# Tile 47's results leave in four transfers of two queues instead of with their neighbours

## The chip, the cores and the metric

The kernel runs on one core of a Trainium2 chip. The metric is the device time of one execution in microseconds. A second figure, the span, is the time from the first to the last instruction of the profiled execution.

## The reference

```python
x, weight, add_value: float32 of (16, 512, 1024), (1024, 768), (16, 512, 768); scale = 0.1

def reference(x, weight, scale, add_value):
    return (scale * np.matmul(x, weight) + add_value).astype(np.float32)
```

It is one product of 8192 x 1024 by 1024 x 768. With all inputs and the output in float32, some 87 MB have to be moved between memory and the core.

## The kernel before

The 8192 rows are cut into 64 tiles of 128 rows. A tile is not 128 neighbouring rows: `BLOCKS` splits the matrix into three blocks of 24, 24 and 16 tiles, and in a block each of the 128 partitions holds so many neighbouring rows, one for each tile. A transfer of n neighbouring tiles therefore moves 128 pieces, one for each partition, of n rows: 4 KB a row for `x`, 3 KB for `add_value` and for the result.

All transfers are issued by SyncE, on one queue, in the order written out by hand in `STREAM` (lines 22 to 25). `x0+4` loads tiles 0 to 3 of `x`, `w0+8` the weight, `a0+8` loads tiles 0 to 7 of `add_value`, and `o32+16` stores the results of tiles 32 to 47. `sync_engine` goes through the list and waits, ahead of each transfer, for what it needs: free slots for a load, finished results for a store. The last entry, `o62+2`, is issued at line 261, after a barrier of all engines that closes the main section (line 255).

On chip the work of a tile goes through these steps:

- `xs` (16 slots) receives tiles of `x`. In `mover`, ScalarE and GpSimd convert them to bf16 into one of two buffers `va`, four tiles at a time: one such step of four is called a move, there are 16, each engine does half of the quadrants of 32 partitions (line 166), and the semaphores `by_act` and `by_pool` count its conversions. The first four moves stand by themselves; the other twelve are a loop of three rounds (line 174).
- VectorE transposes two tiles at a time into `xt` (line 190) and counts `turned`. A move waits for `turned` before it overwrites its buffer.
- TensorE multiplies the transposed tile with the weight, in pieces of 512 and 256 columns (lines 248 and 222), and counts `done`.
- VectorE's `finish` (line 199) takes a pair of tiles, scales the product, adds `ao` (32 slots, into which `add_value` was loaded) and writes the result to the same slots of `ao`. The semaphore `made` counts finished tiles; it starts from the constant `MADE`. There are 32 pairs.

A store of tiles up to `last` waits for `made` to reach `MADE + last`. Tile 47 lies in a slot of `ao` that no later load uses.

Of the kernel before, what the change touches and what calls it, by code (L numbers as in the profile page):

```python
# [7 lines left out]
P = 128  # L8
BLOCKS = ((0, 24), (24, 24), (48, 16))
G = 8  # L10
X_SLOTS = 16
# [5 lines left out]
MOVE = 4  # L17
O_LANES = 4
HALVED = (0, 1)
FETCH = 128  # L20

STREAM = """
    x0+4 w0+8 x4+8 a0+8 x12+4 a8+8 x16+8 a16+8 x24+8 a24+8 x32+8 o0+8 o8+8 a32+8 x40+8
    a40+8 x48+8 x56+4 o16+8 o24+8 a48+4 x60+4 a52+4 a56+8 o32+16 o48+8 o56+6 o62+2
"""


# [7 lines left out]
def kernel(  # L35
# [17 lines left out]
    T = M // P  # L53
# [4 lines left out]
    def blocks(flat):  # L58
        return [(s, g, flat[P * s:P * (s + g), :].rearrange("(p t) n -> p t n", t=g))
                for s, g in BLOCKS]  # L60

    x_v, add_v, out_v = blocks(x_f), blocks(add_f), blocks(out_f)
    w_v = weight.rearrange("(p r) n -> p r n", p=P)

    def rows(view, s, n):
        for first, g, block in view:
            if first <= s and s + n <= first + g:
                return block[:, s - first:s - first + n, :]
        raise ValueError((s, n))
# [5 lines left out]
    ao = const.tile([P, A_SLOTS, N], fp32, name="ao")  # L75
# [10 lines left out]
    by_act, by_pool, pool_go, turned, casts, done, made = (  # L86
        tc.alloc_semaphore(name)
        for name in ("by_act", "by_pool", "pool_go", "turned", "casts", "done", "made"))
    TURNED = MOVE * VA_BUFS
    MADE = TURNED + MM_BUFS  # L90

    def slots(t, n):
        k = (t + G) % A_SLOTS
        assert k + n <= A_SLOTS
        return slice(k, k + n)

    def transfer(eng, op, s, n):
        if op == "w":
            return eng.dma_start(ao[:, s:s + n, :], w_v[:, s:s + n, :])  # L99
        if op == "x":  # L100
            k = s % X_SLOTS
            return eng.dma_start(xs[:, k:k + n, :], rows(x_v, s, n))  # L102
        if op == "a":
            return eng.dma_start(ao[:, slots(s, n), :], rows(add_v, s, n))
        return eng.dma_start(rows(out_v, s, n), ao[:, slots(s, n), :])

    def sync_engine(eng):
        loads, stores, known = [], [], {}

        def need(sem, value):  # L110
            if known.get(id(sem), 0) < value:
                eng.wait_ge(sem, value)
                known[id(sem)] = value

        for op, s, n in stream[:-1]:
            last = s + n
            if op == "w":
                sem = w_sem
            elif op == "x":
                lane = s % X_SLOTS // MOVE  # L120
                if last > X_SLOTS:
                    moved = 8 * (last - X_SLOTS) // MOVE
                    need(by_act, moved)
                    need(by_pool, moved)
                if n == 2 * MOVE:
                    eng.sem_inc(x_sem[lane + 1], 16)
                sem = x_sem[lane]
            elif op == "a":
                if loads:
                    need(a_sem, 16 * len(loads))  # L130
                if slots(s, n).start < KJ:
                    need(casts, KJ)
                if s >= A_SLOTS:
                    for i, (a, b) in enumerate(stores):
                        if a < last - A_SLOTS and s - A_SLOTS < a + b:
                            need(o_sem[i % O_LANES], 16 * (i // O_LANES + 1))
                if s % G:
                    sem = a_late
                else:
                    sem = a_sem  # L140
                    loads.append((s, n))
            else:
                i = len(stores)
                if i >= O_LANES:
                    need(o_sem[i % O_LANES], 16 * (i // O_LANES))
                need(made, MADE + last)
                sem = o_sem[i % O_LANES]
                stores.append((s, n))
            transfer(eng, op, s, n).then_inc(sem, 16)

    def mover(eng, copy, parity, count, go=None):
        if go is None:
            eng.preload_act_table(mybir.ActivationFunctionType.Copy)  # L153

        def move(q, step, landed, freed):
            eng.wait_ge(x_sem[q], landed)
            if freed is not None:
                eng.wait_ge(turned, freed)
            if go is not None:
                eng.sem_inc(go, 1)  # L160
            k = MOVE * q
            src = xs[:, k:k + MOVE, :].rearrange("p i (b k) -> p i b k", b=4)
            for t in range(0, MOVE, step):
                for a in (parity, parity + 2):
                    for b in range(4):
                        copied = copy(va[q % VA_BUFS][32 * b:32 * b + 32, t:t + step, a, :],  # L166
                                      src[32 * a:32 * a + 32, t:t + step, b, :])
                        if step == MOVE or b % 2:
                            copied.then_inc(count, 1)

        for q in range(X_SLOTS // MOVE):
            move(q, MOVE // 2 if q in HALVED else MOVE, 16,
                 MOVE * (q + 1) if q >= VA_BUFS else None)
        with eng.Fori(32, T + 1, X_SLOTS) as i:
            for q in range(X_SLOTS // MOVE):
                move(q, MOVE, i, i + (4 * q - 12) if q < 3 else i)

    def vector_engine(eng):
        ao_g = ao.rearrange("p (g t) n -> p g t n", t=G)
# [73 lines left out]
    for eng in (nc.scalar, nc.gpsimd):  # L253
        eng.addr_align(FETCH, offset=0, max_nops=0)
    with tc.tile_critical(no_gpsimd_drain=True):  # L255
        sync_engine(nc.sync)
        mover(nc.scalar, nc.scalar.copy, 0, by_act)
        mover(nc.gpsimd, nc.gpsimd.tensor_copy, 1, by_pool, pool_go)
        vector_engine(nc.vector)
        tensor_engine(nc.tensor)  # L260
# [36 lines left out]
```

## Time and profile before

| | |
|---|---|
| time, median of 3 runs | 209.57 us (209.47 to 209.66) |
| the profiled execution | 209.42 us, of which the span is 207.6 us |
| granted TensorE clock, mean | 0.978 |
| bytes moved | 87.05 MB, 419 GB/s over the span |
| busy, share of the span | TensorE 82%, GpSimd 67%, ScalarE 66%, VectorE 59% |

Times in quoted rows are microseconds from the start of the span. A row of the timeline gives the start, the duration, the engine and line, the operation, and in brackets the idle time before it and what ended it. A row of a DMA view gives the buffers, the issuing queue, the number of issues, their size and the time from issue to landing; SPq is SyncE's queue, L105 a store, L104 a load of `add_value`, L102 a load of `x`. POOL is GpSimd, DVE VectorE, ACT ScalarE, PE TensorE.

### The profile page before, as it was taken

To read this page: it belongs to the slowest core of one execution; us is meant where nothing else is said; L and a number is where in the kernel's file an instruction comes from. 1 tells how busy PE (TensorE), PEld (TensorE's weight loads), DVE (VectorE), ACT (ScalarE), POOL (GpSimd) and SP (SyncE) were. 2 spreads that over 40 slices of the span, in tenths; PEclk is the share of its full clock that TensorE was granted. 3 is DMA by queue.
4 is the path that set the end of the run, shared out by engine and by line. 5 is a ranking of instruction groups with operands and counts; after the bars stand their busy time and mean duration, and the time that the engine had idled before them with its cause. 6 is when DMAs were issued, how large, how long until landed. Compare 5 with 4: busy or idle time off the path is not lost.

```text
span 207.6 us, 2250 instructions
## 1 busy us (share of the span) xinstructions
PE 170.7 (82%) x1024; PEld 50.8 (24%) x512; DVE 123.0 (59%) x66; ACT 137.8 (66%) x145; POOL 138.3 (67%) x148
## 2 busy tenths in 40 slices
PE   0001993699999999999999999999999899999800
PEld 0000230123223333333333333333333233333200
DVE  0038304937677767776777677767774867777320
ACT  2494199999596969696969079999696959100000
POOL 0399299999797969696969179999796959200000
PEclk9999999699999999999999999999999999999995
DMA  6999999999999999899999999999999999998994
GB/s 224 458 432 410 448 455 404 455 455 404 404 473 436 420 388 505 350 421 440 436 431 447 404 450 459 404 420 436 436 421 428 412 455 469 455 445 355 434 420 173
DMA packets 4034, 87.05 MB, mean 419 GB/s; under 512 B 448, under 2 KB 448, under 8 KB 576
## 3 DMA queue, kind: packets, MB, share of 16 engines
q1 hardware_dynamic: 4032, 87.03, 98.0%
q14 instruction: 2, 0.02, 0.0%
HBM read 61.87 MB, written 25.17 MB: 419 GB/s over the span
## 4 chain that ended last, share of the span: by engine, by line
PE 59%; DMA 26%; POOL 5%; DVE 4%; issue 2%; SPq 0%; DVEq 0%; POOLq 0%
PE mm L248 39%; PE mm L222 20%; DMA xs<-in_x_dram 11%; DMA out_dram<-ao 10%; DMA ao<-in_add_value_dram 5%; POOL va L166 5%; DVE xt L190 2%; DVE ao L199 2%; SPq L99 0%; SPq L102 0%; DVEq L199 0%; DVEq L196 0%; POOLq L160 0%; DVEq L188 0%; SPq L292 0%
## 5 line engine op out<-in xcount | busy, mean ns | idle before, releaser
L248 PE MATMUL mm<-w_bf,xt 128*128 128x512 bf16 x512 | 170.3, 385 | 26.0 <-DVE w_bf L183 20.2
L166 POOL CAST va<-xs 32x1024 bf16<-32x1024 f32 (+1 forms) x144 | 138.1, 959 | 39.1 <-DMA xs<-in_x_dram 18.6
L166 ACT CAST va<-xs 32x1024 bf16<-32x1024 f32 (+1 forms) x144 | 136.5, 948 | 38.4 <-DMA xs<-in_x_dram 20.5
L222 PE MATMUL mm<-w_bf,xt 128*128 128x256 bf16 x512 | 141.4, 276 | 0.0
L199 DVE SCALAR_TENSOR_TENSOR ao<-mm,ao 128x1536 f32 (+1 forms) x32 | 56.2, 1755 | 58.7 <-PE mm L222 46.2
L248 PEld LDWEIGHTS mm<-w_bf,xt 128*128 128x128 bf16 x512 | 50.8, 99 | 145.4 <-issue 138.4
L190 DVE STREAM_TRANSPOSE xt<-va 128x1024 f32<-128x1024 f32 x32 | 65.2, 2037 | 16.9 <-POOL va L166 16.9
L183 DVE CAST w_bf<-ao 128x3072 bf16<-128x3072 f32 x2 | 4.3, 2170 | 0.0
L153 ACT ACT_TABLE_LOAD x1 | 1.3, 1283 | 1.3 <-SPq L255 1.3
L278 POOL MEMSET const-float32-0.0<- 128x1 f32 x1 | 0.1, 98 | 0.2 <-issue 0.2
L278 POOL MEMSET const-bfloat16-1.0<- 128x1 bf16 x1 | 0.1, 100 | 0.0
L278 POOL MEMSET const-uint8-127<- 128x1 uint8 x1 | 0.1, 98 | 0.0
L278 POOL MEMSET const-float32-1.0<- 128x1 f32 x1 | 0.1, 97 | 0.0
## 6 DMA issues: line engine op xcount, KB each, us to landing
xs<-in_x_dram SPq DMA_DIRECT2D x6, 4096.0 KB, 20.5
ao<-in_add_value_dram SPq DMA_DIRECT2D x7, 3072.0 KB, 17.0
out_dram<-ao SPq DMA_DIRECT2D x5, 3072.0 KB, 22.4
xs<-in_x_dram SPq DMA_DIRECT2D x4, 2048.0 KB, 14.3
out_dram<-ao SPq DMA_DIRECT2D x1, 6144.0 KB, 29.9
ao<-in_weight_dram SPq DMA_DIRECT2D x1, 3072.0 KB, 14.0
ao<-in_add_value_dram SPq DMA_DIRECT2D x2, 1536.0 KB, 9.9
out_dram<-ao SPq DMA_DIRECT2D x1, 2304.0 KB, 11.5
```

Source lines behind the costliest of these rows:

```text
L153: eng.preload_act_table(mybir.ActivationFunctionType.Copy)
L166: copied = copy(va[q % VA_BUFS][32 * b:32 * b + 32, t:t + step, a, :], src[32 * a:32 * a + 32, t:t + step, b, :])
L183: eng.tensor_copy(w_bf[:, s:s + n, :], ao[:, s:s + n, :]).then_inc(casts, n)
L190: eng.transpose(xt[:, 2 * half:2 * half + 2, :, :].rearrange("p i c (a m) -> p i c a m", a=4), pairs.rearrange("p i a (k c) -> p i c a k", ...
L199: eng.scalar_tensor_tensor(a, mm[:, q:q + 2, 0:N], float(scale), a, op0=mybir.AluOpType.mult, op1=mybir.AluOpType.add).then_inc(made, 2)
L222: return eng.add_instruction(mybir.InstMatmult(name=nc.get_next_instruction_name(), engine=eng.engine, ins=[eng.lower_ap(weights), eng.low ...
L248: eng.matmul(mm[:, q, 0:CUT], piece, w_bf[:, j, 0:CUT], **flags)
L278: nc = _bacc.Bacc("TRN2", target_bir_lowering=False, num_devices=1)
```

## The change

`o32+16` becomes `o32+15`, and tile 47 is stored by four transfers, cut by rows (partitions): SyncE issues the first 6 rows right after `o32+15`; GpSimd issues the next 5, then 105, then 12. GpSimd does so between its last two moves, once tile 47 is finished. For that the loop of the movers is turned by one: three moves stand ahead of it, a round begins with the fourth, and the last move stands behind it. Each of the four transfers has its own semaphore, and ScalarE waits for all of them at its end. By the change's account the rows are dealt so that DMA engine 4 gets three of the 128.

```diff
+SPREAD = 47
+SPREAD_ROWS = (("SP", 6), ("Pool", 5), ("Pool", 105), ("Pool", 12))
...
-    a40+8 x48+8 x56+4 o16+8 o24+8 a48+4 x60+4 a52+4 a56+8 o32+16 o48+8 o56+6 o62+2
+    a40+8 x48+8 x56+4 o16+8 o24+8 a48+4 x60+4 a52+4 a56+8 o32+15 o48+8 o56+6 o62+2
...
+    spread_sem = [tc.alloc_semaphore(f"spread{i}") for i in range(len(SPREAD_ROWS))]
+
+    def spread(eng, name):
+        first = 0
+        for (by, n), sem in zip(SPREAD_ROWS, spread_sem):
+            if by == name:
+                eng.dma_start(rows(out_v, SPREAD, 1)[first:first + n],
+                              ao[first:first + n, slots(SPREAD, 1), :]).then_inc(sem, 16)
+            first += n
+        assert first == P
...
             transfer(eng, op, s, n).then_inc(sem, 16)
+            if op == "o" and last == SPREAD:
+                need(made, MADE + SPREAD + 1)
+                spread(eng, "SP")
...
-        for q in range(X_SLOTS // MOVE):
+        for q in range(3):
             move(q, MOVE // 2 if q in HALVED else MOVE, 16,
                  MOVE * (q + 1) if q >= VA_BUFS else None)
-        with eng.Fori(32, T + 1, X_SLOTS) as i:
-            for q in range(X_SLOTS // MOVE):
-                move(q, MOVE, i, i + (4 * q - 12) if q < 3 else i)
+        with eng.Fori(16, T, X_SLOTS) as i:
+            move(3, MOVE, i, i)
+            for q in range(3):
+                move(q, MOVE, i + 16, i + 4 * (q + 1))
+        if go is not None:
+            eng.wait_ge(made, MADE + SPREAD + 1)
+            spread(eng, "Pool")
+        move(3, MOVE, T, T)
+        if go is None:
+            for sem in spread_sem:
+                eng.wait_ge(sem, 16)
```

## The prediction

> **What bounds the kernel now.** I began with the page's sums and its lines on DMA, because a kernel that moves 87 MB in 208 us may simply be moving bytes.
>
> ```profile
> span 207.6 us, 2250 instructions
> ...
> DMA packets 4034, 87.05 MB, mean 419 GB/s; under 512 B 448, under 2 KB 448, under 8 KB 576
> ...
> q1 hardware_dynamic: 4032, 87.03, 98.0%
> ```
>
> The sixteen DMA engines are busy 98% of the span, and there is one queue, SyncE's. So every microsecond that an engine of the sixteen moves bytes counts, and compute counts only where it would leave that queue empty. The counts also give the shape of the last transfer: 576 packets under 8 KB less 448 under 512 B are 128 pieces, the 128 rows of o62+2 (two tiles, 6 KB a row), and 128 over 16 engines is 8 each.
>
> Next, who waits at the end: the waits of SyncE from 175 us on.
>
> ```profile
> SPq L292 <- DMA out_dram<-ao: 7.5, 1, 7.5
> SPq L255 <- DVEq L255: 4.7, 1, 4.7
> ```
>
> Line 255 is the barrier after which the last transfer is issued, and it ends with VectorE; line 292 is the end of the program, which waits 7.5 us for stores. So the end is a store landing. How the sixteen engines come to that end is seen in busy time by stretch: width, each engine's busy time, then the TensorE clock, the DMA share and GB/s.
>
> ```profile
> 203.60:204.40 0.80, 0.00 (x0) 0.00 (x0) 0.00 (x0) 0.00 (x0) 0.00 (x0) 0.50 1.02 430
> 204.40:205.09 0.69, 0.00 (x0) 0.00 (x0) 0.00 (x0) 0.00 (x0) 0.00 (x0) 0.50 0.40 162
> 205.09:206.24 1.16, 0.00 (x0) 0.00 (x0) 0.00 (x0) 0.00 (x0) 0.00 (x0) 0.50 0.06 27
> 206.24:207.63 1.39, 0.00 (x0) 0.00 (x0) 0.00 (x0) 0.00 (x0) 0.00 (x0) 0.50 0.00 0
> ...
> 177.00:199.00 22.00, 19.70 (x122) 5.79 (x60) 13.62 (x8) 0.45 (x1) 0.70 (x1) 1.00 0.99 428
> ```
>
> This is the reading on which all else rests. Until 204.40 us all sixteen are busy; from 205.09 to 206.24 the share is 0.06, one sixteenth. One engine alone works for the last 1.16 us. The DMA view of just that stretch counts its packets:
>
> ```profile
> DMA packets 6, 0.03 MB, mean 27 GB/s; under 512 B 1, under 2 KB 1, under 8 KB 6
> ```
>
> Five pieces of 6 KB and one of some bytes: 1.16/5 = 0.23 us for 6 KB, thus 0.115 us for a 3 KB row at that rate. The fifth row of the stretches agrees: 428 GB/s over 16 engines is 26.75 GB/s, and 3,072 B take 0.115 us in large pieces too. No other engine starts a piece after 205.09, so every other one has ended by 205.32. The late one is 0.92 to 1.16 us behind, and the end of the program waits for it alone.
>
> **The change, part by part.** (1) *Rows.* Tile 47 leaves o32+16, which becomes 15 tiles, and its 128 rows of 3 KB go out in transfers of 6, 5, 105 and 12 rows. The bytes stay the same; who carries them changes. By the change's own account engine 4 gets three rows instead of eight. The remaining 125 over fifteen engines are 8.3 each: dealt evenly, six rows go to six engines, five to five, 105 to fifteen by seven, and twelve to twelve, so the others get 8 or 9. Let p be the price of a row as a piece of its own. Engine 4: -8 x 0.115 + 3p. Another engine: -0.92 + 8p or 9p. No 3 KB piece stands in this trace. Its lower bound is 0.115 (half the 6 KB piece), its upper 0.23 (as long as the 6 KB one). I take 0.12, since 48 KB and 6 KB pieces cost the same for each byte to 1%, so there is little fixed cost to see. Then engine 4 gains 0.92 - 0.36 = **0.56 us**, and the others lose 0.04 to 0.16.
>
> What is late next: if the late engine is number 4 it ends at 206.24 - 0.56 = 205.68; the others by 205.32 + 0.16 = 205.48. The late engine still ends last, so its whole 0.56 us shows.
>
> The trace gives no engine its number; that the late one is number 4 is an assumption of the change that I can't read here.
>
> (2) *SyncE.* One more wait and one more issue, after o32. Its issues:
>
> ```profile
> 162.08 0.43 SPq L105 DMA_DIRECT2D out_dram<-ao  x1
> 177.82 0.34 SPq L105 DMA_DIRECT2D out_dram<-ao  x1
> 198.84 0.33 SPq L105 DMA_DIRECT2D out_dram<-ao  x1
> ```
>
> The added issue costs some 0.43 us at 162.5, and the next (o48, at 177.82) follows 15 us later: cost nothing. The wait is for the product of tile 47, which VectorE finishes in pair 24 of 32:
>
> ```profile
> 154.34 1.76 DVE L199 SCALAR_TENSOR_TENSOR ao<-mm,ao 128x1536 f32 x1 [1.48 <-PE mm L222]
> ```
>
> The groups of VectorE from 156.2 us on count what follows:
>
> ```profile
> L199 DVE SCALAR_TENSOR_TENSOR ao<-mm,ao 128x1536 f32 (+1 forms) x8 | 14.1, 1757 | 14.9 <-PE mm L222 11.4 <-DMA ao<-in_add_value_dram 3.5
> ```
>
> Eight pairs. So the pair at 154.34 is number 24, tile 47 is done at 156.1, and neither SyncE at 162.5 nor GpSimd, ten microseconds later than that, waits. The six rows stand in SyncE's ring behind o32.
>
> (3) *GpSimd.* Three issues between the moves of tiles 56 to 59 and 60 to 63; behind them in its queue is the last move, for which VectorE's transposes wait.
>
> ```profile
> 158.21 8.70 POOL L166 CAST va<-xs 32x1024 bf16<-32x1024 f32 x8 [1.68 <-DVE xt L190]
> 169.00 8.70 POOL L166 CAST va<-xs 32x1024 bf16<-32x1024 f32 x8 [2.10 <-DVE xt L190]
> ```
>
> ```profile
> 182.91 2.00 DVE L190 STREAM_TRANSPOSE xt<-va 128x1024 f32<-128x1024 f32 x1
> ```
>
> GpSimd is free from 166.91 and would idle 2.10 us anyway until VectorE has freed the buffer. The move then ends at 177.70, and its first reader starts at 182.91: 5.2 us more. Three issues may take 7.3 us, 2.4 each, before anything is later. No row shows a GpSimd issue. From below SyncE's 0.33 us is the nearest, from above GpSimd's own 1.09 us for an instruction on 32 rows (8.70/8): 1 to 3.3 us for three, below 7.3. Cost nothing; without that cover, the excess over 7.3 us would come one for one on VectorE's path.
>
> The three transfers then move at about 168 to 176 us, beside o32 and a56:
>
> ```profile
> ao<-in_add_value_dram SPq DMA_DIRECT2D x1, 3072.0 KB, 15.5
> ...
> out_dram<-ao SPq DMA_DIRECT2D x1, 6144.0 KB, 29.9
> ...
> out_dram<-ao SPq DMA_DIRECT2D x1, 768.0 KB, 7.9
> ```
>
> a56 is issued at 161.61 and lands at 177.1. Rows that go in between push it by at most 9 x 0.12 = 1.1 us, to 178.2; its reader is the pair just before the transpose at 182.91, at 181.2. Hidden, by 3 us.
>
> (4) *The moves' loop* now begins at its fourth move, so its branch stands elsewhere: the same moves and waits, and the converters idle before the late moves as shown. (5) *ScalarE* waits at its end for all four transfers, and through the barrier at line 255 so does the last issue at 198.84. o32 lands at 162.08 + 29.9 = 192.0 and the six rows by then too; the other three much earlier. Cost nothing, with 6.6 us to spare.
>
> **Sum.** The profiled execution took 209.42 us (207.6 of span and 1.8 around it): 209.42 - 0.56 = 208.86. The median of the runs is 209.57, 0.15 higher, and the difference carries over: **209.0 us**. 0.2% of it, 0.42 us, is about what a measurement of this kernel can tell from no change; the gain lies only little over it.
>
> **The rivals.** *A, the last issue waits (slower).* If DMA engines serve SyncE's backlog first and GpSimd's queue only when it is empty, tile 47 moves after o56. Each engine takes 8 x 0.23 = 1.84 us for o62, so o56 ends on most engines at 205.09 - 1.84 = 203.3 or earlier. Eight rows of 0.12 make that 204.2; landing takes 206.7 (198.84 + 7.9) less 206.24, some 0.48: 204.7. From VectorE's end at 198.56 to the issue at 198.84 the barrier takes 0.28: issued at 205.0. A first transfer needs about a microsecond to move, as the start of the program shows: SyncE's first issue stands at 0.94, and
>
> ```profile
> 0.94:1.74 0.80, 0.00 (x0) 0.00 (x0) 0.00 (x0) 0.43 (x1) 0.00 (x0) 1.00 0.00 0
> ```
>
> in the 0.8 us after it nothing moves. So 206.0 + 1.84 + 0.48 = 208.3, 1.6 us later than now, and up to 2.5 with the late engine's own delay: about 211.5 us. It decides from the point where one of the four lands after 198.56 us. For it: nothing yet shows how two queues share. Against: the landing would have to slip by over 20 us.
>
> *B, dealt otherwise.* If the 105 rows go seven each to the first fifteen engines and the 12 to the first twelve, engine 4 gets 1 + 1 + 7 + 1 = 10 rows, +1.20 - 0.92 = +0.28: 209.85 us. For it: nothing in the diff names an engine. Against: the change's own count. [...]
>
> *C, another engine is late.* Then it gets 8 or 9 rows, +0.04 to +0.16: 209.6 to 209.7 us. For it: the trace shows one late engine without its number. [...]
>
> *D, small pieces are dear.* At p = 0.23 the others get 9 x 0.23 - 0.92 = +1.15 and end at 206.24 to 206.47, as late as engine 4 was: 209.6 to 209.8 us. Against: bytes, not pieces, set the price from 48 KB down to 6.
>
> **How the numbers follow.** Forecast 0.58, A 0.14, B 0.11, C 0.10, D 0.07. The forecast's own range is 208.8 to 209.2 (p from 0.115 to 0.15, and 0.1 for the spread of runs), and 0.04 of its chance falls within 0.42 us of no change: faster 0.54. Same: that 0.04, most of B (0.09), C (0.10) and most of D (0.05), 0.28. Slower: A and the rest, 0.18. The range leaves out A and takes in the others: 208.7 to 209.9 us.
>
> **What would show it.** Right: the stretch in which one sixteenth of the DMA share works at the end shrinks from 1.16 to some 0.45 us; o62 lands about 0.56 us earlier after its issue, still at 198.8; GpSimd's last move starts at 169 to 171 and VectorE's transposes where they were. Wrong: the lone stretch stays or grows by two rows (B, C); it fills up with all engines (D); or line 255's wait ends with ScalarE, not VectorE (A).

## The result and the profile after

| | before | after |
|---|---|---|
| median, 22 runs each | 209.43 us | 209.78 us |
| lowest and highest | 209.29, 209.74 | 209.53, 210.25 |
| profiled execution | 209.42 us, span 207.6 | 209.96 us, span 208.2 |

The ratio after to before is 1.0016, with a 95% interval of 1.0009 to 1.0022: the change costs some 0.35 us, where a gain of 0.56 was forecast. That is under 0.2%, but the whole interval lies above 1: it is a small loss. The two profiled executions differ by 0.54 us; 0.18 of that is there already when a52 lands (169.98 after, 169.80 before, by the last engine's count on its semaphore), before any row of tile 47 has moved.

The page after, its DMA queues and GpSimd's new issues:

```profile
DMA packets 4190, 87.05 MB, mean 418 GB/s; under 512 B 521, under 2 KB 521, under 8 KB 732
...
q1 hardware_dynamic: 4044, 86.66, 97.4%
q0 software_dynamic: 144, 0.38, 0.5%
...
L115 POOL DMA_DIRECT2D out_dram<-ao x3 | 1.7, 576 | 0.0
```

There is a second queue now, q0, with 0.38 MB: the 122 rows that GpSimd issues. An issue took GpSimd 0.58 us, between the bounds of 0.33 and 1.09. GpSimd's and VectorE's timeline at that place:

```profile
167.19 1.71 POOL L115 DMA_DIRECT2D out_dram<-ao  x3
169.22 8.69 POOL L182 CAST va<-xs 32x1024 bf16<-32x1024 f32 x8 [0.33 <-issue]
```

```profile
183.13 2.02 DVE L214 STREAM_TRANSPOSE xt<-va 128x1024 f32<-128x1024 f32 x1
```

The last move begins at 169.22 instead of 169.00 and is read at 183.13 instead of 182.91. The whole compute side is 0.22 us later. ScalarE's last move, which has no issue ahead of it, is later by the same amount (169.15 instead of 168.93), so GpSimd's three issues lie in the idle time that covered them and cost nothing. The waits of SyncE at the end are the same two:

```profile
SPq L316 <- DMA out_dram<-ao: 7.8, 1, 7.8
SPq L279 <- DVEq L279: 4.7, 1, 4.7
```

The barrier (line 279 now) still ends with VectorE, not with ScalarE and its added waits: rival A is out. GpSimd's transfers did not starve either; the DMA view from 160 to 178 us gives their times to landing (POOLq):

```profile
out_dram<-ao POOLq DMA_DIRECT2D x1, 315.0 KB, 10.7
out_dram<-ao POOLq DMA_DIRECT2D x1, 36.0 KB, 13.6
...
out_dram<-ao POOLq DMA_DIRECT2D x1, 15.0 KB, 6.0
```

All of them land by 182 us, 17 us ahead of the end of the barrier. What did change is the end, in busy time by stretch:

```profile
203.60:204.40 0.80, 0.00 (x0) 0.00 (x0) 0.00 (x0) 0.00 (x0) 0.00 (x0) 0.50 0.97 407
204.40:205.19 0.79, 0.00 (x0) 0.00 (x0) 0.00 (x0) 0.00 (x0) 0.00 (x0) 0.50 0.49 202
205.19:206.75 1.56, 0.00 (x0) 0.00 (x0) 0.00 (x0) 0.00 (x0) 0.00 (x0) 0.50 0.06 24
```

The stretch in which one sixteenth of the DMA share is at work did not shrink to 0.45 us; it grew from 1.16 to 1.56. (By the single packets the other engines end at 205.16 before and 205.19 after, so the time alone is 1.09 and then 1.56 us.) The others end where they ended; the late engine ends half a microsecond later, at 206.75 instead of 206.25. That was the sign named for B and C.

**Reading each engine's share out of the trace.** The packets have no engine number, but in the busy part of the trace an engine's next packet starts 3 to 4 ns before the end of its last. Packets can be strung together by this. In the trace before, from 177.2 us on, every one of the sixteen strings holds eight 24 KB pieces of o48 and eight 18 KB pieces of o56; eight pieces a string are taken for every 128-row transfer of SyncE, which settles most doubtful places. In the trace after, from 169 us on, the string that ends last (206.75) holds three 3 KB pieces and three 6 KB pieces of GpSimd's queue and one 3 KB piece of SyncE's: **ten rows** of tile 47, not three. One string holds none at all, and it is the one that ends first, at 204.49. So the change did relieve one engine, and of all eight rows, but not the late one.

### The profile page after: what moved, and what is told of

It reads as the page before. It is cut to its first block, busy times and chain, and to the rows that moved or that the text cites. A ratio compares the mean times of both kernels' runs of the same rounds, so it can differ in the third digit from the quotient of the medians.

```text
span 208.2 us, 2247 instructions
## 1 busy us (share of the span) xinstructions
PE 170.5 (82%) x1008; PEld 50.8 (24%) x512; DVE 122.5 (59%) x66; ACT 137.8 (66%) x145; POOL 140.2 (67%) x151
## 4 chain that ended last, share of the span: by engine, by line
PE 58%; DMA 26%; POOL 5%; DVE 4%; issue 2%; SPq 0%; DVEq 0%; POOLq 0%
PE mm L272 38%; PE mm L246 21%; DMA xs<-in_x_dram 11%; DMA out_dram<-ao 10%; DMA ao<-in_add_value_dram 5%; POOL va L182 5%; DVE xt L214 2%; DVE ao L223 2%; SPq L101 0%; SPq L104 0%; DVEq L223 0%; DVEq L220 0%; POOLq L176 0%; DVEq L212 0%; SPq L316 0%
## 5 line engine op out<-in xcount | busy, mean ns | idle before, releaser
L272 PE MATMUL mm<-w_bf,xt 128*128 128x512 bf16 x496 | 166.6, 386 | 25.6 <-DVE w_bf L207 19.8
L207 DVE CAST w_bf<-ao 128x3072 bf16<-128x3072 f32 x2 | 3.8, 1936 | 0.0
L115 POOL DMA_DIRECT2D out_dram<-ao x3 | 1.7, 576 | 0.0
```

Of the source, the lines that this page charges most:

```text
L115: eng.dma_start(rows(out_v, SPREAD, 1)[first:first + n], ao[first:first + n, slots(SPREAD, 1), :]).then_inc(sem, 16)
L207: eng.tensor_copy(w_bf[:, s:s + n, :], ao[:, s:s + n, :]).then_inc(casts, n)
L272: eng.matmul(mm[:, q, 0:CUT], piece, w_bf[:, j, 0:CUT], **flags)
```

## The experiments

Each time is compared with the kernel before, run beside it. Each edit is to the changed kernel; where a cut shows only a `+` line, it stands in the place of the changed kernel's line of that name, and the remarks behind `#` are not in the code. How many rows an engine carries is read from the strings of the run's trace. Theory: GpSimd's transfers are dealt from the first engine on, so the late one gets ten rows (rival B of the prediction). Rivals: GpSimd's queue itself costs the time; the turned loop does; the late engine is another one (C).

**e1_all_sync.** The same rows without GpSimd.

```diff
-SPREAD_ROWS = (("SP", 6), ("Pool", 5), ("Pool", 105), ("Pool", 12))
+SPREAD_ROWS = (("SP", 6), ("SP", 5), ("SP", 105), ("SP", 12))
```

> The same four groups of rows (6, 5, 105, 12), all issued by SyncE, none by GpSimd. Theory of the dealing: engine 4, the late one, gets one row of each group it takes part in and seven of the 105, ten in all instead of eight, whichever queue issues them; a row inside o32's large pieces takes 0.1135 us, a row alone 0.121, so 10 x 0.121 - 8 x 0.1135 = +0.30 us, ratio to before 1.0014, as with the changed kernel (1.0016). The lone engine's stretch at the end grows by about 0.3 us less what the others gain. Theory of the queue (GpSimd's transfers are themselves what costs, by their own packets and by the interleaving of two queues): without them about +0.05 us, ratio 1.0002. [...]

Measured: 209.82 us against 209.46, ratio 1.0012 (1.0003 to 1.0022), the loss of the changed kernel without a single issue of GpSimd. Its strings come out cleanly:

| rows of tile 47 | 10 | 9 | 8 | 7 | 0 |
|---|---|---|---|---|---|
| engines | 5 | 1 | 6 | 3 | 1 |

That is just what 6, 5, 105 (seven each) and 12 rows give if every transfer starts with the same first engine. The late engine is one of the five with ten. The trace has no engine numbers; what the counts show is that all four transfers start with the same first engine.

**e2_pool_whole.** All of tile 47 by GpSimd, eight rows an engine.

```diff
+SPREAD_ROWS = (("Pool", 128),)
```

> All 128 rows of tile 47 in one transfer of GpSimd, none by SyncE. Theory of the dealing: eight rows for every engine, so only the price of smaller pieces is left: 8 x (0.121 - 0.1135) = +0.06 us, ratio 1.0003. Theory of the queue: as many rows move by GpSimd's queue as in the changed kernel, so the loss stays near +0.3 us, ratio 1.0014 or more.

Measured: 209.51 against 209.46, ratio 1.0000 (0.9992 to 1.0009). GpSimd's queue shows no cost of its own, and neither do its small pieces: here each engine's eight rows leave as four pieces of 6 KB. The queue as cause is out.

**e5_loop_only.** The turned loop alone: o32+16 whole, no split, no added waits.

> The movers' loop turned by one as in the changed kernel, but o32+16 whole and no split transfer, no added wait. Theory of the dealing: the loop costs nothing, ratio 1.0000 within the interval. Rival (the loop's branch at another place, and the code behind it, cost the 0.35 us): ratio 1.0015.

Measured: 209.40 against 209.48, ratio 0.9994 (0.9985 to 1.0003). The loop shows no cost.

**e3_four and e4_five.** Which engine is late. SyncE alone; the short transfers reach the first four engines, or the first five.

```diff
+SPREAD_ROWS = (("SP", 96),) + 8 * (("SP", 4),)                  # e3_four
+SPREAD_ROWS = (("SP", 96),) + 6 * (("SP", 5),) + (("SP", 2),)   # e4_five
```

> SyncE alone: 96 rows in one transfer (six for each of 16 engines), then eight transfers of four rows (one row each for the first four engines, 0 to 3). Engines 0 to 3 get 14 rows, all others 6. If the late engine is number 4 (or any above 3): 6 x 0.121 - 8 x 0.1135 = -0.18 us, ratio 0.9991; engines 0 to 3 lose 14 x 0.121 - 0.91 = 0.79 us and still end before it, so the stretch that one engine works alone shrinks to a few tenths. If it is one of 0 to 3: +0.79 us, ratio 1.0038, and the lone stretch grows to about 1.9 us. The theory of the queue expects nothing of itself here, as GpSimd issues none.

> SyncE alone: 96 rows, then six transfers of five rows (engines 0 to 4) and one of two (engines 0 and 1). Engine 4 gets 12 rows, engines 0 to 3 12 or 13, engines 5 to 15 six. If the late engine is number 4: 12 x 0.121 - 0.91 = +0.54 us, ratio 1.0026, while the run with four rows to a transfer gains: the two together then name engine 4. If it is above 4: -0.18 us, ratio 0.9991. If it is one of 0 to 3: +0.54 to +0.67, and the run with four would lose too.

Measured: e3_four 209.63 against 209.46, ratio 1.0010 (0.9998 to 1.0022); e4_five 210.84, ratio 1.0067 (1.0055 to 1.0079). Neither figure fits what was expected. Pieces of tile 47 ran slowly here: in each run eight 3 KB pieces took 0.08 to 0.66 us over their 0.121, nearly 2 us in sum over the engines.

But the strings tell which engine is which. In e3_four two strings with 14 rows end last, at 206.42 and 206.53, and a string with six rows stands at 205.71, well above the others with six (204.25 to 205.18): the late engine, not among the first four. (It ends 0.36 us sooner than the expected 0.18 below 206.25. The late engine's lag varies from trace to trace: at 157.5 us, ahead of anything that these edits move, it is 0.11 us here and 0.22 to 0.49 in the others. That may be part of it, and it is why sizes are taken from the medians of many runs here, not from one trace.) In e4_five a string with 12 rows ends alone:

```profile
205.61:207.57 1.96, 0.00 (x0) 0.00 (x0) 0.00 (x0) 0.00 (x0) 0.00 (x0) 0.50 0.06 25
```

So it is among the first five and not among the first four. Counted from 0 in the order of the dealing it is number 4, as the change has it, and C is out. The next two runs say the same with hardly a slow piece: the string that ends last holds three rows in e7 and eight in e8, while the first four engines get eight in both.

**e7_three_rows and e8_eight_rows.** What three rows on engine 4 would have brought. The two differ on engine 4 alone. Both leave rows of tile 47 unstored (60 in e7, 55 in e8), so they give a price and are no versions of the kernel.

```diff
+SPREAD_ROWS = (("SP", 48),) + 5 * (("SP", 4),)   # e7: engine 4 three rows, 0 to 3 eight
+SPREAD_ROWS = (("SP", 48),) + 5 * (("SP", 5),)   # e8: engines 0 to 4 eight
-        assert first == P
```

> What the change meant for engine 4, by leaving rows out: SyncE stores 48 rows of tile 47 (three for each engine) and five transfers of four rows (engines 0 to 3); the other 60 rows of tile 47 are not stored. Engine 4 has three rows, engines 0 to 3 eight, engines 5 to 15 three. Theory of the dealing: engine 4 sets the end, so 3 x 0.121 - 8 x 0.1135 = -0.55 us, ratio 0.9974, though engines 0 to 3 carry as much as before. Rival (the end is set by something else than the rows of one engine, such as the barrier or the pace of all): less than 0.2 us, ratio 0.999 or more.

> The partner of the run with three rows: 48 rows and five transfers of five rows (engines 0 to 4), 55 rows of tile 47 not stored. Only engine 4 differs from that run, by five rows: eight instead of three. Theory of the dealing: back to 8 x 0.121 - 8 x 0.1135 = +0.06 us, ratio 1.0003, and up to +0.8 us more if the small transfers meet a stall as in the run with 12 rows on that engine; 0.6 us or more above its partner. Rival (another engine is late, or the end is set elsewhere): the same as its partner.

Measured: three rows 209.07 against 209.48, ratio 0.9983 (0.9974 to 0.9992); eight rows 209.57, ratio 1.0004 (0.9995 to 1.0013). Five rows on one engine of sixteen are worth 209.57 - 209.07 = 0.50 us of the whole time, a little under the 0.6 expected. Three rows against the eight of the kernel before, the case of the prediction's sum, gained 0.41 us where the sum has 0.56. The last stretches, e7 and then e8:

```profile
204.93:205.74 0.81, 0.00 (x0) 0.00 (x0) 0.00 (x0) 0.00 (x0) 0.00 (x0) 0.50 0.11 46
```

```profile
204.95:206.34 1.39, 0.00 (x0) 0.00 (x0) 0.00 (x0) 0.00 (x0) 0.00 (x0) 0.50 0.05 22
```

With eight rows one engine works alone for 1.39 us. With three it is two engines (share 0.11) for 0.81: number 4 ends at 205.74, half a microsecond before its 206.25 in the kernel before, and one of the first four, with a 3 KB piece that took 0.43 too long, ends at 205.72. Relief beyond that would have shown nothing in this run: the next engine is there.

**Versions that store everything.** Since every transfer seen here begins with the same first engine, no mix of them takes rows from engine 4 alone; what can be done is to move some from engines 4 to 15 to the first four.

```diff
+SPREAD_ROWS = (("SP", 112),) + 4 * (("SP", 4),)   # e6: tile 47; e9: tiles 46, 47; e10: 45 to 47
...
```

> SyncE alone, all rows stored: 112 rows (seven for each engine), then four transfers of four rows (engines 0 to 3). Engine 4 gets 7 rows, engines 0 to 3 get 11. Theory of the dealing, with the late engine being number 4: 7 x 0.121 - 8 x 0.1135 = -0.06 us at the least, and engines 0 to 3 gain about 0.5 us and stay below it: ratio 0.999 to 1.000. In the run with eight transfers of four, two of the engines 0 to 3 had a single 3 KB piece of 0.78 us; if such a stall comes from many small transfers, four of them should give fewer or none. If it falls on an engine here again, ratio 1.000 to 1.001.

Measured: 209.36 against 209.48, ratio 0.9993 (0.9984 to 1.0002): the right size for one row less, but not told apart from no change.

> A version meant to beat both, all rows stored: o32+14 and then tiles 46 and 47 together by SyncE, 112 rows (seven 6 KB pieces for each engine) and four transfers of four rows (engines 0 to 3). Engine 4 has seven 6 KB pieces instead of eight: -0.23 us; engines 0 to 3 have eleven, +0.69 us, and end near 205.2 + 0.7 = 205.9 at the latest, just below engine 4's 206.0. Theory of the dealing: -0.1 to -0.23 us, ratio 0.9989 to 0.9995. Where a stall of a small piece (0.8 us in the run with eight transfers of four rows) falls on one of the engines 0 to 3, that engine ends at 206.5 or so and the ratio is 1.000 to 1.001.

> The same with tiles 45 to 47 and 9 KB pieces: engine 4 -0.34 us, engines 0 to 3 +1.03 us each, which brings the last of them to 206.2, past engine 4's 205.9. Theory of the dealing: the end passes to one of the engines 0 to 3, ratio 0.999 to 1.000, no better than with two tiles. If engine 4 were still last, ratio 0.9984.

Measured: two tiles 209.80 against 209.50, ratio 1.0023 (1.0012 to 1.0035); three tiles 211.18, ratio 1.0079 (1.0066 to 1.0092). Both missed, on the losing side. Eleven 6 KB pieces took 0.2 to 0.8 us over their 0.23, and nineteen 9 KB pieces up to 1.1 over their 0.35: 4.1 and 9.6 us in sum. In the stretch of the short transfers the engines are busy at a full share but move fewer bytes than the 428 GB/s that the kernel before moved at a share of 0.99 from 177 to 199 us. With two tiles and then with three:

```profile
188.50:191.50 3.00, 3.00 (x20) 0.88 (x9) 1.63 (x1) 0.00 (x0) 0.00 (x0) 1.00 1.07 412
```

```profile
188.50:191.50 3.00, 3.00 (x21) 0.90 (x10) 1.85 (x1) 0.00 (x0) 0.00 (x0) 1.00 1.06 391
```

**e11_two_apart and e12_three_apart.** Whether neighbouring partitions do that.

```diff
+                part = slice(0, n) if n > 4 else slice(112 + first, P, 4)
...
-            first += n
-        assert first == P
+            first = first + 1 if n == 4 else 0
```

> As the run with two tiles, but each transfer of four rows takes partitions four apart (112, 116, 120, 124; then 113, 117 and so on) instead of four neighbours. In the run with neighbours, eleven 6 KB pieces of the short transfers took 0.2 to 0.8 us over their usual 0.23. Theory of the neighbours (four engines that read neighbouring partitions at once slow each other): the slow pieces go, engine 4 has -0.23 us, engines 0 to 3 +0.69 and stay below it: ratio 0.9989 to 0.9995. Rival (short transfers are slow as such, whichever partitions they take): as with neighbours, 1.002. [...]

> As the run with three tiles, with partitions four apart. Theory of the neighbours: engines 0 to 3 have +1.03 us without slow pieces and end at 206.2 at the latest, engine 4 at 205.9: ratio 0.999 to 1.000. Rival (short transfers are slow as such): as with neighbours, 1.008.

Measured: two tiles 210.63 against 209.44, ratio 1.0055 (1.0037 to 1.0073); three tiles 210.31, ratio 1.0040 (1.0027 to 1.0053). With three tiles the slow pieces fell from nineteen to eleven and their excess from 9.6 to 3.7 us, and the loss halved; with two tiles the excess fell too, from 4.1 to 2.4 us, and the time rose. The trace of e11 shows where the excess fell. The transfer of 112 rows lands on its last engine at 192.98 us, 2.13 us behind the next, while o32 ahead of it had a lag of 0.90. That is the late engine. It has no part in the short transfers, which had all landed by 192.13, but its seven 6 KB pieces took 3.0 us, from 189.64 to 192.65, instead of 1.6. So pieces that moved beside the short transfers were slow too, on the very engine that sets the end. The choice of partitions changes the time, but the simple theory of neighbours doesn't hold: it expected the slow pieces to go. What slows them stays open. Of the versions that store everything, none was found that beats the kernel before by more than can be measured.

## Why the prediction was wrong

- **What bounds the kernel: right.** One late DMA engine sets the end. e7 and e8 show it: five rows on that engine move the whole time by 0.50 us, though no other engine carries more or less.
- **(1) Rows: the step that failed.** "By the change's own account engine 4 gets three rows instead of eight." It gets ten. The size was taken over where the price was worked out, and the sum hangs on it: with ten rows the same prices give the +0.28 us of rival B, and 0.35 was measured. B had a chance of 0.11. The reason given against it was the change's own count, which is a statement of intent and not a row. The diff held the other answer: nothing in it names an engine, and 105 rows that go seven each to fifteen engines in a row pass over engine 4 only where their dealing starts behind it. The trace after agrees with B, 105 rows dealt from the first engine on, seven each to fifteen: the late string holds ten rows, and one string holds none at all.
- **The late engine is number 4: right**, an assumption then, shown by e3 and e4 together. Rival C is out. Engine 4 is late without any transfer of GpSimd: the kernel before, where its lag at the end is 1.14 us, has none, and neither have e3 and e4, which name it.
- **The price of a row alone, 0.12 us: right** for the changed kernel, whose 3 KB pieces took 0.121. A row inside a large piece was put a little high: the 48 KB pieces of the kernel before took 1.815 us, 0.113 for a row and not 0.115, while a 6 KB piece took 0.234, which is 3% more for each byte and not 1%. Rival D is out there. Dear pieces come back, for a reason that stays open, in short transfers of SyncE and beside them (e1, e3, e4, e7, e9 to e12).
- **What is late next: hardly tested.** In e7 engine 4 still ended last, but only by 0.02 us, since a slow piece held up one of the first four. Most other engines carried three rows there, not 8 or 9, so no run shows the 205.48 of the prediction.
- **(2) to (5): right.** SyncE's issue took 0.37 us (0.43 said) and GpSimd's three 1.71 (1 to 3.3), both hidden. a56 took 16.6 us to land instead of 15.5, the 1.1 allowed for it. The loop costs nothing (e5), and neither do ScalarE's waits, of which e6 has five.
- **The chances: badly weighed.** Forecast and B rested on the same working and differed in one fact that no row of the trace of before could show. Between them the chances should have stood much nearer to each other. That the measured 209.78 us lies between the stated 208.7 and 209.9 is no merit of the forecast, whose own range ended at 209.2: the wider one held it because it took in B.

## What to carry to other kernels

Where a transfer is cut unevenly to balance DMA engines, find out first who carries what: string the packets of a trace together, or make two runs that differ on one engine alone, before any time is worked out from the deal. Transfers of SyncE and GpSimd both began with the same first engines here, so uneven row counts could spare the last engines, but not one in the middle alone. The size of such a gain is bounded by the stretch at the end in which one sixteenth of the DMA share is at work, and the next engine behind it.

## What was not expected of the hardware

One engine of the sixteen falls behind, and mostly while stores are moved. In the trace of before the last engine's lag behind the next, by the counts on the semaphores, is 0.01 us at 137.5, 0.45 at 157.5, 0.58 at 177.1 and 1.14 at the end. It grows while o16 and o24, then o32 and o48 are moved, and keeps its size over the loads from 161.2 to 177.1 us. Over the last two stores, o56 and o62, it doesn't grow either (1.13 at 199.4). In o48 its 24 KB pieces took 0.92 to 0.96 us, those of the others 0.91. What slows it isn't shown. Of the 122 rows that GpSimd issues in the changed kernel, 90 left as 45 pieces of 6 KB, two rows each, and 32 as pieces of 3 KB. And some small pieces in short transfers on four or five engines, or beside them, were slow out of proportion: a 6 KB piece took up to 1.06 us instead of 0.23, and a 9 KB piece up to 1.46 instead of 0.35.
